# Turning 32x32 blocks into whole transposes: a round trip through DRAM against sixteen direct transfers inside SBUF

## The chip, the core and the metric

The kernel runs on one core of one Trainium2 chip. The time is the device time of one execution in microseconds (us), and lower is better. The core has TensorE (PE) for matrix products, with its own row for weight loads (PEld), VectorE (DVE), ScalarE (ACT), GpSimd (POOL) and SyncE (SP), which here only issues transfers. PE writes to the accumulation memory PSUM; everything else lies in the on-chip memory SBUF (128 partitions) or in DRAM.

## What is computed

Two layers over x of shape (1, 256, 2048): h = h + Mixer(RMSNorm(h)). Layer A is a gated DeltaNet, layer B a banded softmax attention. Both have 16 heads of 128 features, one wide input projection (8224 and 8192 columns) and an output projection of 2048 x 2048. Cut to its core, the reference is:

```python
def gated_deltanet(h, ...):                       # layer A
    proj = h @ w_in
    qkv = silu(causal_depthwise_conv(proj[..., :6144], conv_w))
    q, k, v = heads of qkv;  q, k = l2_norm(q), l2_norm(k)
    # chunks of 64: decay products, a unit lower triangular solve, a scan over chunks
    o = rms_norm(o, out_norm_w) * silu(z)
    return o @ w_out

def chunk_band_attention(h, ...):                 # layer B
    q, k = rms_norm(heads), rms_norm(heads);  v, z = proj parts
    s = q @ k.T * scale + bias[relative distance]  # own chunk and 8 before it
    o = softmax(s) @ v
    return (o * silu(z)) @ w_out
```

Everything is float32. The kernel splits each weight tile and each activation into a high part (float32r) and the rest, and adds three products.

## The kernel before

**The weight stream.** The list `plan` (L137 to L159) holds all weight tiles, 512 KB each, in order of use; one tile with its matmuls is called a chunk, and `state["use"]` counts them. For each chunk SP loads a tile into `wt` (four buffers, L203), ACT copies its high part to `whi` (L204) and DVE writes the rest to `wlo` (L205); both have three buffers. PE then runs 12 products of width 512 in a "tokens" chunk, whose result has tokens on partitions, or 16 in a "half" chunk (widths 512 and 256), whose result has features on partitions (L253).

**The work between.** All other work is written as generators in two lanes, `bgq` and `bg2`. `tick` and `step` (L225 to L246) advance one of them by one step after a part of each chunk, so their instructions are emitted between the matmuls. `until(n)` holds a generator until chunk n has been reached; such numbers are called distances here. A planner orders the instructions of each engine when the program is built (L1375): it simulates the engines and takes, in the order of emission, what it believes to be ready. On the chip each engine then runs its list strictly in order, and waits at an instruction whose data are not there.

**The turn.** In several places a [tokens, features] array has to become [features, tokens] or the reverse. DVE's transpose turns 32x32 blocks in place of a whole 128x128 transpose, so the blocks lie transposed but on the wrong partitions: block (r, c) still stands at partition group r and has to go to partition group c. Before the change this is done by `trip` (L410), where POOL writes the whole array to a DRAM buffer, and `back` (L417), where SP reads it in four transfers, one for each group of 32 partitions:

```python
nc.gpsimd.dma_start(out=m, in_=u.rearrange("p x c j -> p c (x j)"))            # trip
nc.sync.dma_start(out=dst[32 * c:32 * c + 32].rearrange("i r x j -> i r (x j)"),  # back, c = 0..3
                  in_=m[:, c, :].rearrange("(r i) y -> i r y", r=4))
```

Between the two stands a distance, and another one between `back` and the instruction that reads the result. There are 29 such turns: four in `v_conv` (layer A's values; the turned blocks lie in the tile `raw`, of which there is one, and `v_turn` at L859 reads the result), two in `ha_land` (first layer's output, L1023), four in `zb_small` (layer B's gates; `z`), eight in `qk_norm` (k straight into `kn`; q into a landing tile that ACT scales into `qn`, L1148), eight in `attend` (the softmax weights of two heads at a time; the turned blocks lie in one single buffer, `st["u"]`, which L1193 writes) and three in `out_land` (the last output, L1294). The landing tiles have the tag `cv`, which has two buffers. In `attend` a head goes through the stages scores, weights, turned and fetched_, two chunks apart. POOL also computes the powers that the norms need: `rn` (L1124) in `qk_norm`, `ro` (L907) in `v_gate`.

Of the kernel before, what the change touches and what calls it, by code (L numbers as in the profile page):

```python
# [7 lines left out]
F32 = mybir.dt.float32  # L8
# [6 lines left out]
P = 128  # L15
# [24 lines left out]
def tile_hybrid_trunk(  # L40
# [11 lines left out]
    nc = tc.nc  # L52
# [13 lines left out]
    def wk(tag, bufs=None):  # L66

        return work.tile([P, 4, T], F32, name=tag, tag=tag, bufs=bufs)
# [91 lines left out]
    fetched, splits, state = {}, {}, {"next": 0, "use": 0, "mm": None}  # L160
# [52 lines left out]
    bgq, bg2, now = [], [], []  # L213
# [191 lines left out]
    beta = ht("beta")  # L405
    rows = ctx.enter_context(tc.tile_pool(name="rows", bufs=1, space=bass.MemoryType.DRAM))

    trips = [0]

    def trip(u):  # L410

        trips[0] += 1
        m = rows.tile([P, 4, 32 * u.shape[1]], F32, name="trip%d" % trips[0])
        nc.gpsimd.dma_start(out=m, in_=u.rearrange("p x c j -> p c (x j)"))  # L414
        return m

    def back(dst, m):  # L417

        for c in range(4):
            nc.sync.dma_start(out=dst[32 * c:32 * c + 32].rearrange("i r x j -> i r (x j)"),  # L420
                              in_=m[:, c, :].rearrange("(r i) y -> i r y", r=4))

    def until(use):

        while state["use"] < use:
            yield 0
# [108 lines left out]
    def conv(src, i0):  # L535

        raw = wk("raw", 1)
        scaled(raw, src, scales["x"][1])
        cv = wk("cv")
        yield cv  # L540
        for i in range(4):
            act.activation(out=cv[:, i, :], in_=raw[:, i, :], func=AF.Copy, scale=conv_w(i0 + i, 3))  # L542
            for s in (1, 2, 3):
                dve.scalar_tensor_tensor(out=cv[:, i, s:], in0=raw[:, i, :T - s], scalar=conv_w(i0 + i, 3 - s),  # L544
                                         in1=cv[:, i, s:], op0=ALU.mult, op1=ALU.add)
            yield cv
# [280 lines left out]
    def v_conv(gi, ps):  # L827
        for n, cv in enumerate(conv(ps, 32 + 4 * gi)):
            if n in (2, 4):
                act.activation(out=cv[:, n - 2:n], in_=cv[:, n - 2:n], func=AF.Silu)  # L830
            yield 1
        u = wk("raw", 1).rearrange("p h t -> p (h t)").rearrange("p (c x j) -> p x c j", c=4, j=32)
        for n in (0, 2):
            dve.transpose(out=u[:, 2 * n:2 * n + 4],
                          in_=cv[:, n:n + 2].rearrange("p h (t c i) -> p (h t) c i", t=2, c=4))
            yield 1
        m, end = trip(u), state["use"]
        yield from until(end + 4)
        while vmem["turned"] < gi - 1:
            yield 0  # L840
        land = wk("cv").rearrange("p h t -> p (h t)").rearrange("p (r x j) -> p r x j", r=4, j=32)
        back(land, m)
        vmem[gi] = land
        yield 1

# [169 lines left out]

    def ha_land(ks, u, end):
        yield from until(end)
        m, end = trip(u), state["use"]
        yield from until(end + 4)
        land = wk("cv").rearrange("p h t -> p (h t)").rearrange("p (r x j) -> p r x j", r=4, j=32)  # L1020
        back(land, m)
        yield from until(end + 7)
        h = hmem["h"][:, ks, :].rearrange("p k (t r j) -> p (k t) r j", t=2, r=4)  # L1023
        dve.tensor_tensor(out=h, in0=land.rearrange("p r x j -> p x r j"), in1=h, op=ALU.add)
        yield 1
        yield from ha_split(ks)
# [15 lines left out]
    bmem = {}  # L1042
# [36 lines left out]
    def zb_small(gi, ps, end):  # L1079
        n, u = wk("cv").rearrange("p h t -> p (h t)").rearrange("p (t d) -> p t d", t=2), blocks(8)  # L1080
        for t in range(2):
            act.activation(out=n[:, t, :], in_=ps[:, t, :], func=AF.Silu, scale=scales["h"][0][:, t:t + 1])
        yield 1

        bias, hs = bmem["bias"], slice(4 * gi, 4 * gi + 4)
        dve.tensor_copy(out=bias[0:1, 4 * gi, 0:1], in_=n[0:1, 0, 0:1])
        nc.gpsimd.dma_start(out=bias[:, hs, :], in_=relb[:, hs, :])
        pool.memset(bias[0:64, hs, 192:256], NEG)
        yield 1
        for t in range(2):  # L1090
            turn_tokens(u, t, n[:, t, :])
            yield 1
        m = trip(u)
        yield from until(end + 4)
        back(bmem["z"][:, gi], m)
        yield 1

    while "x" not in hmem:
        step()
# [10 lines left out]
    for j in (2, 3):  # L1110
        bgq.append(zb_small(j, block("tokens", xb, 2), state["use"]))

    def qk_norm(ps, scale, dst, end):

        ssn = tiny.tile([P, 2, 4], F32, name="ssn", tag="so")
        rn = tiny.tile([P, 2, 4], F32, name="rn", tag="ro")
        sq = wk("cv").rearrange("p h t -> p (h t)")
        act.activation(out=sq, in_=ps.rearrange("p t d -> p (t d)"), func=AF.Square)
        yield from until(end + 1)
        dve.reduce_sum(out=ssn, in_=sq.rearrange("p (t h d) -> p t h d", t=2, d=P), axis=AX.X)  # L1120
        for t in range(2):
            pool.tensor_scalar(out=ssn[:, t, :], in0=ssn[:, t, :], scalar1=1.0 / P, scalar2=bmem["uh"][:, t:t + 1],
                               op0=ALU.mult, op1=ALU.add)
        pool.tensor_tensor(out=rn, in0=ssn, in1=nhalf[:, :8].rearrange("p (t h) -> p t h", t=2), op=ALU.pow)  # L1124
        yield from until(end + 3)
        n = wk("cv").rearrange("p h t -> p (h t)").rearrange("p (t d) -> p t d", t=2)
        for t in range(2):
            dve.tensor_tensor(out=n[:, t, :].rearrange("p (h d) -> p h d", d=P),
                              in0=ps[:, t, :].rearrange("p (h d) -> p h d", d=P),
                              in1=rn[:, t, :].unsqueeze(2).broadcast_to([P, 4, P]), op=ALU.mult)  # L1130
        yield 1
        u = wk("cv").rearrange("p h t -> p (h t)").rearrange("p (c x j) -> p x c j", c=4, j=32)
        for t in range(2):
            dve.transpose(out=u[:, 4 * t:4 * t + 4], in_=n[:, t, :].rearrange("p (x c i) -> p x c i", c=4, i=32))
            yield 1
        m = trip(u)
        yield from until(end + 6)
        if scale is None:
            back(dst, m)
            yield 1  # L1140
            return
        g = wk("cv").rearrange("p h t -> p (h t)").rearrange("p (r x j) -> p r x j", r=4, j=32)
        back(g, m)
        yield from until(end + 10)
        while bmem["scored"] < bmem["turned"]:
            yield 0
        bmem["turned"] += 1
        act.activation(out=dst.rearrange("p x (r j) -> p r x j", r=4), in_=g, func=AF.Copy, scale=scale)  # L1148
        yield 1

    def attend(gi, qn, kn, end):
# [5 lines left out]
        st = {}  # L1157
# [31 lines left out]
        def turned(i):  # L1189
            if i % 2 == 0:  # L1190
                st["u"] = hmem["m"][:, 11264:12032].rearrange("p (c x j) -> p x c j", c=4, j=32)
            x = 3 * (i % 2)
            dve.transpose(out=st["u"][:, x:x + 3], in_=st[i][0].rearrange("p (x c i) -> p x c i", c=4, i=32))  # L1193
            if i % 2:
                st["m", i] = trip(st["u"])

        def fetched_(i):
            if i % 2:
                back(weights_of((4 * gi + i) // 2), st["m", i])

        stages = (scores, weights, turned, None, None, fetched_)
        while bmem["turned"] <= gi:
            yield 0
        for n in range(4 + len(stages) - 1):
# [8 lines left out]
    def weights_of(pr):  # L1213

        w = bmem["w"][:, 768 * pr:768 * pr + 768] if pr < 5 else hmem["m"][:, 2 * D + 768 * (pr - 5):2 * D + 768 * (pr - 4)]
        return w.rearrange("p (r x j) -> p r x j", r=4, j=32)
# [31 lines left out]
    for gi in range(4):  # L1248
        c = 1024 * (gi % 2)
# [30 lines left out]
    def out_turn(j, ps, end):  # L1280
        u = blocks(8)
        for t in range(2):
            turn_tokens(u, t, ps[:, t, :])
        yield 1
        bg2.append(out_land(j, trip(u), end))

    def out_land(j, m, end):
        yield from until(end + 3)
        land = wk("cv").rearrange("p h t -> p (h t)").rearrange("p (r x j) -> p r x j", r=4, j=32)
        back(land, m)  # L1290
        yield from until(end + 6)
        ks = slice(4 * j, 4 * j + 4)
        h = h_r[:, ks, :].rearrange("p k (t r j) -> p (k t) r j", t=2, r=4)
        dve.tensor_tensor(out=h, in0=land.rearrange("p r x j -> p x r j"), in1=h, op=ALU.add)  # L1294
        nc.sync.dma_start(out=ov[:, ks], in_=h_r[:, ks, :])
        yield 1
# [82 lines left out]
```

## Time and profile before

| | us |
|---|---|
| median of 3 runs (lowest to highest) | 976.91 (975.65 to 978.31) |
| the profiled execution | 974.92 |
| its span in the profile | 973.2 |
| busy: PE, DVE, ACT, POOL | 967.4, 702.3, 519.7, 91.4 |
| granted TensorE clock in the profiled execution | 1.00 |

The span is what the profile's rows are counted in; 1.7 us of the profiled execution lie outside it. In the rows, "L253" is a line of the kernel, "x24" a count, and "a<-b" says that a is written from b. A wait "X <- Y" is idle time of X that ended when Y was done. "SPq" rows are the transfer commands on SP's list, and their duration is the time that a command takes to issue, not the transfer; the time from issue to landing has its own column.

### The profile page before, as it was taken

The page shows a single profiled execution, that of the slowest core. Times are in us where ns is not written, and L with a number is a line of the kernel's source. Part 1 is how long each engine was busy: PE and PEld are TensorE (multiplying, and loading weights), DVE is VectorE, ACT ScalarE, POOL GpSimd, SP SyncE. Part 2 cuts the span into 40 slices and gives each one's busy share as a digit, 9 for nine tenths or more (in the row PEclk, how much of TensorE's full clock was granted, in tenths as well). Part 3 has the DMA queues.
Part 4 walks back from the last instruction along what each step waited for, and adds up shares of the span by engine and source line. Part 5 has one row for each costly group of instructions (what it writes and reads, how often), then busy time and mean ns, then how long its engine had stood idle before and what let it go on. Part 6 is the DMA issues. An engine that isn't in the chain of part 4 may idle for free.

```text
span 973.2 us, 14443 instructions
## 1 busy us (share of the span) xinstructions
PE 967.4 (99%) x5355; PEld 825.4 (85%) x5355; DVE 702.3 (72%) x1147; ACT 519.7 (53%) x731; POOL 91.4 (9%) x126
## 2 busy tenths in 40 slices
PE   9999999999999999999999999999999999999998
PEld 7988888888888889888888888888888888888887
DVE  7789787998899877866686555566767676655464
ACT  8465887655546556544564444445454545444332
POOL 1002100122000000101001000111212120000000
PEclk9999999999999999999999999999999999999999
DMA  9667765645675665566966798788898987665694
GB/s 297 195 168 230 231 197 164 179 128 177 175 195 150 179 204 165 170 192 193 301 201 199 225 286 291 212 250 259 234 288 246 275 249 208 203 191 173 204 308 151
DMA packets 144934, 207.93 MB, mean 214 GB/s; under 512 B 10320, under 2 KB 87008, under 8 KB 144864
## 3 DMA queue, kind: packets, MB, share of 16 engines
q1 hardware_dynamic: 139152, 186.28, 64.9%
q0 software_dynamic: 5424, 20.47, 6.0%
q8 instruction: 42, 0.69, 0.3%
q10 hardware_dynamic: 288, 0.26, 0.1%
q14 instruction: 28, 0.23, 0.1%
HBM read 190.71 MB, written 16.27 MB: 213 GB/s over the span
## 4 chain that ended last, share of the span: by engine, by line
PE 94%; DVE 2%; ACT 1%; DMA 1%; issue 1%; SPq 0%; DVEq 0%; ACTq 0%
PE psp L253 85%; PE pss L627 2%; PE pss L253 1%; PE pss L872 1%; PE pss L1166 1%; PE pss L1235 1%; DMA trip<-raw 1%; DVE wlo L205 1%; DVE cv L544 1%; DMA g<-in_xT_dram 1%; PE pss L893 0%; PE pss L894 0%; PE pss L895 0%; PE pss L879 0%; PE pss L1237 0%
## 5 line engine op out<-in xcount | busy, mean ns | idle before, releaser
L205 DVE TENSOR_TENSOR wlo<-wt,whi 128x1024 fp32r<-128x1024 f32 (+2 forms) x324 | 390.0, 1207 | 206.7 <-ACT whi L204 201.8
L204 ACT CAST whi<-wt 128x1024 fp32r<-128x1024 f32 (+2 forms) x324 | 336.6, 1040 | 366.6 <-PE psp L253 301.8
L253 PE MATMUL psp<-whi,xb 128*128 128x512 f32 x1280 | 402.2, 392 | 0.0
L253 PEld LDWEIGHTS psp<-whi,xb 128*128 128x128 f32 x1280 | 240.0, 188 | 49.2
L253 PE MATMUL psp<-wlo,xb 128*128 128x512 f32 x640 | 249.8, 390 | 0.0
L253 PE MATMUL psp<-xb,whi 128*128 128x512 f32 (+1 forms) x832 | 196.2, 376 | 0.5 <-ACT whi L204 0.5
L253 PEld LDWEIGHTS psp<-xb,whi 128*128 128x128 f32 x832 | 148.2, 189 | 25.2 <-ACT whi L204 0.7
L253 PEld LDWEIGHTS psp<-wlo,xb 128*128 128x128 f32 x640 | 120.2, 188 | 24.6
L253 PE MATMUL psp<-xb,wlo 128*128 128x256 f32 x768 | 113.4, 285 | 0.5 <-DVE wlo L205 0.4
L253 PEld LDWEIGHTS psp<-xb,wlo 128*128 128x128 f32 x768 | 103.3, 191 | 5.0 <-DVE wlo L205 1.1
L253 PE MATMUL psp<-whi,g 128*128 128x512 f32 x320 | 99.5, 390 | 0.0
L253 PEld LDWEIGHTS psp<-whi,g 128*128 128x128 f32 x320 | 60.1, 188 | 12.3
L544 DVE SCALAR_TENSOR_TENSOR cv<-raw,sm,cv 128x255 f32<-128x255 f32 (+2 forms) x144 | 64.3, 480 | 2.4 <-ACT cv L542 2.0
L253 PE MATMUL psp<-wlo,g 128*128 128x512 f32 x160 | 62.7, 392 | 0.0
L253 PE MATMUL psp<-g,whi 128*128 128x512 f32 x160 | 38.5, 391 | 0.0
L253 PEld LDWEIGHTS psp<-wlo,g 128*128 128x128 f32 x160 | 30.0, 188 | 6.2 <-DVE wlo L205 0.3
L253 PEld LDWEIGHTS psp<-g,whi 128*128 128x128 f32 x160 | 29.4, 188 | 5.7
L542 ACT ACTIVATE cv<-raw,sm 128x256 f32<-128x256 f32 x48 | 22.2, 501 | 18.7 <-DVE raw L339 18.7
L414 POOL DMA_DIRECT2D trip<-cv x17 | 9.8, 576 | 147.5 <-DVE cv L434 117.4
L1179 ACT ACTIVATE raw<-raw,mx 128x128 f32<-128x128 f32 (+1 forms) x32 | 14.4, 449 | 16.7 <-DVE mx L1177 16.7
L253 PEld LDWEIGHTS psp<-g,wlo 128*128 128x128 f32 x160 | 20.5, 191 | 0.8
L253 PE MATMUL psp<-g,wlo 128*128 128x256 f32 x160 | 20.8, 283 | 0.0
(251 smaller groups left out, 788.4 us busy)
## 6 DMA issues: line engine op xcount, KB each, us to landing
wt<-in_b_w_in_dram SPq DMA_DIRECT2D x128, 512.0 KB, 4.5
wt<-in_a_w_in_dram SPq DMA_DIRECT2D x125, 512.0 KB, 4.1
wt<-in_a_w_out_dram SPq DMA_DIRECT2D x32, 512.0 KB, 4.9
wt<-in_b_w_out_dram SPq DMA_DIRECT2D x32, 512.0 KB, 4.5
trip<-cv POOLq DMA_DIRECT2D x17, 512.0 KB, 4.5
cv<-trip SPq DMA_DIRECT2D x52, 128.0 KB, 5.0
trip<-dl POOLq DMA_DIRECT2D x8, 384.0 KB, 4.4
tt<-line POOLq DMA_DIRECT2D x4, 512.0 KB, 8.5
```

Of the source, the lines that this page charges most:

```text
L204: cast = act.copy(out=hi[:, js, cs], in_=wt[:, js, cs])
L205: rest = dve.tensor_tensor(out=lo[:, js, cs], in0=wt[:, js, cs], in1=hi[:, js, cs].bitcast(F32), op=ALU.subtract)
L253: state["mm"] = pe.matmul(*args, **kw).ins
L414: nc.gpsimd.dma_start(out=m, in_=u.rearrange("p x c j -> p c (x j)"))
L542: act.activation(out=cv[:, i, :], in_=raw[:, i, :], func=AF.Copy, scale=conv_w(i0 + i, 3))
L544: dve.scalar_tensor_tensor(out=cv[:, i, s:], in0=raw[:, i, :T - s], scalar=conv_w(i0 + i, 3 - s), in1=cv[:, i, s:], op0=ALU.mult, op1=ALU.add)
L627: pe.matmul(dst, lhsT=kq[:, a, i, c:c + P], rhs=rhs, start=(n == 0), stop=(n == 2))
L872: pe.matmul(ps[:, i * P:(i + 1) * P], lhsT=tt[:, 2 * (h0 + i) + t, :], rhs=vb[:, i, t, :], start=True, stop=True)
L1166: pe.matmul(ps[:, 128:384].rearrange("p (t r j) -> p t r j", t=2, j=32), lhsT=q1, rhs=kb, start=True, stop=True)
L1179: act.activation(out=s[:, a:b], in_=s[:, a:b], func=AF.Exp, bias=mx[:, t:t + 1], accum_out=sums[:, t:t + 1])
L1235: pe.matmul(ps[:, 0:256].rearrange("p (x r j) -> p x r j", x=2, j=32), lhsT=v[:, 0, vs], rhs=pT0, start=True, stop=False)
```

## The change

`trip`, `back` and the 29 DRAM buffers go. `regroup` takes their place: for each pair (r, c) one transfer moves the block straight from partition group r of the turned array to partition group c of the destination, 32 partitions with one contiguous run each (1 KB, or 768 B in `attend`). The 16 transfers go in turn to SP and to POOL, eight each. `regroup` is itself a generator: it emits four transfers, then gives the turn back, four times; only `attend` emits all 16 at once. The distances between trip and back fall away, and those before the consumer become shorter where there are any (q: `end + 8` for `end + 10`; output: `end + 5` for `end + 6`; first layer's output: three chunks after the transfers were emitted). In `attend` the stage `fetched_` is gone, and the transfers are issued in the stage `turned`, three stages earlier.

```diff
--- before.py
+++ after.py
@@ -405,20 +405,12 @@
     beta = ht("beta")
     rows = ctx.enter_context(tc.tile_pool(name="rows", bufs=1, space=bass.MemoryType.DRAM))
 
-    trips = [0]
-
-    def trip(u):
-
-        trips[0] += 1
-        m = rows.tile([P, 4, 32 * u.shape[1]], F32, name="trip%d" % trips[0])
-        nc.gpsimd.dma_start(out=m, in_=u.rearrange("p x c j -> p c (x j)"))
-        return m
-
-    def back(dst, m):
-
-        for c in range(4):
-            nc.sync.dma_start(out=dst[32 * c:32 * c + 32].rearrange("i r x j -> i r (x j)"),
-                              in_=m[:, c, :].rearrange("(r i) y -> i r y", r=4))
+    def regroup(dst, u):
+
+        for r in range(4):
+            for c in range(4):
+                (nc.sync, nc.gpsimd)[(r + c) % 2].dma_start(out=dst[32 * c:32 * c + 32, r], in_=u[32 * r:32 * r + 32, :, c])
+            yield 1
 
     def until(use):
 
@@ -834,12 +826,10 @@
             dve.transpose(out=u[:, 2 * n:2 * n + 4],
                           in_=cv[:, n:n + 2].rearrange("p h (t c i) -> p (h t) c i", t=2, c=4))
             yield 1
-        m, end = trip(u), state["use"]
-        yield from until(end + 4)
         while vmem["turned"] < gi - 1:
             yield 0
         land = wk("cv").rearrange("p h t -> p (h t)").rearrange("p (r x j) -> p r x j", r=4, j=32)
-        back(land, m)
+        yield from regroup(land, u)
         vmem[gi] = land
         yield 1
 
@@ -1015,11 +1005,9 @@
 
     def ha_land(ks, u, end):
         yield from until(end)
-        m, end = trip(u), state["use"]
-        yield from until(end + 4)
         land = wk("cv").rearrange("p h t -> p (h t)").rearrange("p (r x j) -> p r x j", r=4, j=32)
-        back(land, m)
-        yield from until(end + 7)
+        yield from regroup(land, u)
+        yield from until(state["use"] + 3)
         h = hmem["h"][:, ks, :].rearrange("p k (t r j) -> p (k t) r j", t=2, r=4)
         dve.tensor_tensor(out=h, in0=land.rearrange("p r x j -> p x r j"), in1=h, op=ALU.add)
         yield 1
@@ -1090,10 +1078,7 @@
         for t in range(2):
             turn_tokens(u, t, n[:, t, :])
             yield 1
-        m = trip(u)
-        yield from until(end + 4)
-        back(bmem["z"][:, gi], m)
-        yield 1
+        yield from regroup(bmem["z"][:, gi], u)
 
     while "x" not in hmem:
         step()
@@ -1133,15 +1118,12 @@
         for t in range(2):
             dve.transpose(out=u[:, 4 * t:4 * t + 4], in_=n[:, t, :].rearrange("p (x c i) -> p x c i", c=4, i=32))
             yield 1
-        m = trip(u)
-        yield from until(end + 6)
         if scale is None:
-            back(dst, m)
-            yield 1
+            yield from regroup(dst, u)
             return
         g = wk("cv").rearrange("p h t -> p (h t)").rearrange("p (r x j) -> p r x j", r=4, j=32)
-        back(g, m)
-        yield from until(end + 10)
+        yield from regroup(g, u)
+        yield from until(end + 8)
         while bmem["scored"] < bmem["turned"]:
             yield 0
         bmem["turned"] += 1
@@ -1192,13 +1174,10 @@
             x = 3 * (i % 2)
             dve.transpose(out=st["u"][:, x:x + 3], in_=st[i][0].rearrange("p (x c i) -> p x c i", c=4, i=32))
             if i % 2:
-                st["m", i] = trip(st["u"])
-
-        def fetched_(i):
-            if i % 2:
-                back(weights_of((4 * gi + i) // 2), st["m", i])
-
-        stages = (scores, weights, turned, None, None, fetched_)
+                for _ in regroup(weights_of((4 * gi + i) // 2), st["u"]):
+                    pass
+
+        stages = (scores, weights, turned, None, None, None)
         while bmem["turned"] <= gi:
             yield 0
         for n in range(4 + len(stages) - 1):
@@ -1282,13 +1261,12 @@
         for t in range(2):
             turn_tokens(u, t, ps[:, t, :])
         yield 1
-        bg2.append(out_land(j, trip(u), end))
-
-    def out_land(j, m, end):
-        yield from until(end + 3)
+        bg2.append(out_land(j, u, end))
+
+    def out_land(j, u, end):
         land = wk("cv").rearrange("p h t -> p (h t)").rearrange("p (r x j) -> p r x j", r=4, j=32)
-        back(land, m)
-        yield from until(end + 6)
+        yield from regroup(land, u)
+        yield from until(end + 5)
         ks = slice(4 * j, 4 * j + 4)
         h = h_r[:, ks, :].rearrange("p k (t r j) -> p (k t) r j", t=2, r=4)
         dve.tensor_tensor(out=h, in0=land.rearrange("p r x j -> p x r j"), in1=h, op=ALU.add)
```

## The prediction

> **What bounds the kernel now.** I read the busy table first, then the table by stretches, to see whether the full PE hides gaps.
>
> ```profile
> span 973.2 us, 14443 instructions
> PE 967.4 (99%) x5355; PEld 825.4 (85%) x5355; DVE 702.3 (72%) x1147; ACT 519.7 (53%) x731; POOL 91.4 (9%) x126
> ```
>
> ```profile
> 300.00:320.00 20.00, 20.00 (x218) 17.44 (x218) 19.52 (x29) 13.84 (x18) 2.75 (x3) 1.00 0.52 139
> 320.00:340.00 20.00, 19.89 (x360) 16.91 (x359) 16.43 (x28) 10.30 (x18) 0.00 (x0) 1.00 0.60 182
> 340.00:460.00 120.00, 120.00 (x724) 104.73 (x723) 87.74 (x141) 65.10 (x91) 10.07 (x9) 1.00 0.60 182
> 560.00:580.00 20.00, 20.00 (x90) 16.57 (x89) 10.07 (x10) 7.89 (x9) 0.84 (x2) 1.00 0.95 293
> 700.00:720.00 20.00, 20.00 (x90) 16.57 (x89) 13.34 (x16) 9.70 (x10) 4.22 (x5) 1.00 1.01 299
> 960.00:973.00 13.00, 9.79 (x62) 8.69 (x61) 6.14 (x9) 1.62 (x3) 0.00 (x0) 1.00 0.24 82
> ```
>
> The columns are stretch, length, then busy time and count of PE, PEld, DVE, ACT and POOL, the granted clock, the transfer engines' share and GB/s. PE works through every stage in which a turn happens: 0.11 us idle between 300 and 460 us, none at 560 or at 700. Of the 5.8 us that PE is idle in all (973.2 - 967.4), 3.2 lie in the last stretch, at the kernel's end. So whatever becomes earlier can give back almost nothing; the question is which delay reaches PE.
>
> Where would it? In the chain of waits one turn lies on the path:
>
> ```profile
> 318.05 6.10 DMA trip<-raw
> 324.24 0.70 DVE raw L339
> ...
> 337.29 4.91 PE psp L253 x25
> ```
>
> Start, duration, work. Between 300 and 320 us DVE is 19.52 of 20 busy, because the triangular solve's end, the values' convolution and the weight split meet there. DVE stands at L339 until the single tile `raw` has been read out to DRAM, and from there the path runs through DVE's list back to PE's stream at 337.29. The other stages have a reserve, read from DVE's and ACT's lists in order of time:
>
> ```profile
> 690.88 0.57 DVE L1193 STREAM_TRANSPOSE dl<-raw 128x384 f32<-128x384 f32 x1
> 696.12 1.29 DVE L1128 TENSOR_TENSOR cv<-psp,rn 128x512 f32<-128x512 f32 x2 [1.16 <-POOL rn L1124]
> 698.46 0.57 DVE L1193 STREAM_TRANSPOSE dl<-raw 128x384 f32<-128x384 f32 x1
> 700.20 1.19 DVE L205 TENSOR_TENSOR wlo<-wt,whi 128x1024 fp32r<-128x1024 f32 x1
> 709.22 1.22 DVE L205 TENSOR_TENSOR wlo<-wt,whi 128x1024 fp32r<-128x1024 f32 x1 [1.49 <-ACT whi L204]
> ```
> ```profile
> 697.29 1.06 ACT L204 CAST whi<-wt 128x1024 fp32r<-128x1024 f32 x1 [0.79 <-ACT raw L1179]
> 705.41 1.05 ACT L204 CAST whi<-wt 128x1024 fp32r<-128x1024 f32 x1 [1.66 <-PE psp L253]
> 708.13 1.05 ACT L204 CAST whi<-wt 128x1024 fp32r<-128x1024 f32 x1 [1.67 <-PE psp L253]
> 571.64 2.16 ACT L204 CAST whi<-wt 128x1024 fp32r<-128x1024 f32 x2 [3.94 <-DMA wt<-in_b_w_in_dram]
> ```
>
> A chunk takes 2.72 us (705.41 to 708.13). A cast begins when PE frees one of three buffers, so its tile is needed two chunks later: 708.13 + 5.44 = 713.57. DVE's part of it is done at 710.44, which is 3.1 us early. A weight that came 3.94 us late (571.64) cost PE nothing: the stretch 560 to 580 shows 20.00. So delays of up to about 3 us on DVE, and of 4 us on a load, are covered.
>
> **The change, part by part.** The prices:
>
> ```profile
> L414 POOL DMA_DIRECT2D trip<-cv x17: 533/559/617, 462.9 to 949.1; - x17
> L414 POOL DMA_DIRECT2D trip<-dl x8: 542/544/550, 691.8 to 847.3; - x8
> L414 POOL DMA_DIRECT2D trip<-raw x4: 531/566/682, 318.1 to 408.3; - x4
> L420 SPq DMA_DIRECT2D cv<-trip x52: 303/430/1442, 324.2 to 954.5; - x52
> L859 DVEq EVENT_SEMAPHORE  x8: 21/36/50, 329.8 to 417.6; - x8
> ```
> ```profile
> trip<-cv POOLq DMA_DIRECT2D x17, 512.0 KB, 4.5
> kT<-trip SPq DMA_DIRECT2D x20, 96.0 KB, 3.3
> line<-kT POOLq DMA_DIRECT2D x1, 16.0 KB, 2.8
> ```
> ```profile
> SPq L420 <- DMA trip<-cv: 36.5, 17, 4.6
> SPq L420 <- DMA trip<-dl: 11.7, 8, 2.0
> SPq L420 <- DMA trip<-raw: 9.0, 4, 4.6
> ```
>
> The first fence has minimum, median and maximum in ns of an issue; the second KB each and the median us from issue to landing; the third SP's waits in all, their number, the longest.
>
> *Removed:* 29 POOL issues and 116 SP issues, SP's 57.2 us of standing (36.5 + 11.7 + 9.0) with weight loads queued behind it, and half the bytes: 21 x 512 KB + 8 x 384 KB out and the same back become one move. *Worth:* nothing. SP's longest stand, 4.6 us, is inside the reserve of a load, and PE shows no gap there.
>
> *Added on SP:* 232 issues for 116, that is 8 x 0.43 = 3.4 us a turn instead of 1.7. A load behind them is at most 3.4 us later, less than the covered 3.94. They wait for DVE's transposes instead of a landing. Price 0, covered by four weight buffers; without that cover 3.4 us a turn.
>
> *Added on POOL:* 232 issues for 29. A turn takes POOL 8 x 0.56 = 4.5 us instead of 0.56, in all 203 x 0.56 = 114 us on an engine with 91.4 busy. That matters where the last piece's landing is waited for, or where POOL owes DVE something. No row shows a 32 KB piece's landing; the bounds are 2.8 us (16 KB from POOL) and 4.5 us (512 KB from POOL). I take 3.3, the 96 KB row, which is the nearest one out of this pattern.
>
> *First values turn (318 us, on the path).* Last piece starts 7 x 0.566 = 4.0 us after the first and lands 3.3 later: 7.3 us instead of 6.10, so +1.2 (bounds 4.0 + 2.8 - 6.1 = +0.7 and 4.0 + 4.5 - 6.1 = +2.4). The consumer now collects 16 completions instead of one; at 36 ns per collecting instruction 15 more are 0.5 us on DVE. Together **+1.7**, bounds 0 (the planner puts other DVE work first, and the wait has no one behind it) and +2.9. The later three values turns land earlier than before (no DRAM hop), so these waits shrink:
>
> ```profile
> DVE dl L859 <- DMA cv<-trip: 8.0, 3, 4.2
> DVE raw L339 <- DMA trip<-raw: 3.2, 1, 3.2
> ```
>
> At PE's 120.00 of 120 the 8.0 us are worth nothing.
>
> The Trainium skill ("DMA: Bandwidth & Descriptors", Rules for kernel authors) speaks against the change: it says to coalesce small transfers, because under 64 KB one pays mostly overhead, and the same page (Anatomy of one DMA, SWDGE path) puts about 2.0 us of fixed cost on each transfer. As an estimate from that page a 32 KB piece lands in 2.1 us; since pieces overlap, this term would be 4.0 + 2.1 - 6.1 + 0.5 = +0.5 and the sum, by the profiled execution's time, 974.9 + 0.5 = 975.4. Were the 2 us paid one after another, a turn's eight pieces would hold POOL's queue for 17 us; the 16 KB row's 2.8 us is of the first kind, and no run here shows pieces in a row.
>
> *Attention turns (eight, `attend`).* All 16 pieces are emitted at once, and the single buffer `st["u"]` is written again two chunks later. I price this at 0 in the forecast, because the planner draws DVE's list anew and may put the rewrite behind weight splits; the upper bound is the first rival.
>
> *Gates, q and k, outputs.* In the gates POOL's pieces stand behind a memset that waits for a bias load, and the next gate's transposes reuse the buffer two chunks later:
>
> ```profile
> 558.84 0.31 POOL L1088 MEMSET dl<- 64x256 f32 x1 [4.08 <-DMA dl<-in_relb_dram]
> 560.18 0.71 DVE L434 STREAM_TRANSPOSE cv<-cv 128x512 f32<-128x512 f32 x1 [2.05 <-DMA trip<-cv]
> ```
>
> The transposes already stand 2.05 us here; with eight pieces behind 558.84 the last lands 0.3 + 4.0 + 3.3 us on, at 566.4. That would be 6 us more if the next gate came as early as now, but it is emitted only after the four steps of `regroup`, some two chunks later, so I count no loss (bound +2.5). Elsewhere the pieces go out two per step and engine, and readers come two chunks (5.4 us) or more behind the last piece, against 3.3 to 4.5 of landing. Shorter distances put them at the edge, so waits of 1 to 2 us may appear on DVE or ACT; the 3.1 us cover them. Price 0; without cover 15 such turns would cost up to 2 us each.
>
> **Sum:** 974.92 (the profiled execution: span 973.2 and 1.7 around it) + 1.7 = 976.6. The median of the runs is 976.91, 2.0 above that execution, so the forecast is 976.91 + 1.7 = **978.6**.
>
> **Rivals.** *First, slower: POOL's queue in the attention stage.* The rows that collide:
>
> ```profile
> 691.75 0.55 POOL L414 DMA_DIRECT2D trip<-dl  x1 [16.11 <-DVE sums L1185]
> 692.73 1.61 POOL L1122 TENSOR_SCALAR ssn<-ssn,uh 128x4 f32<-128x4 f32 x2 [0.42 <-DVE ssn L1120]
> 694.42 1.66 POOL L1124 TENSOR_TENSOR rn<-ssn,nhalf 128x8 f32<-128x8 f32 x1
> ```
>
> One issue stands right before the power `rn`, for which DVE already waits 1.16 us at 696.12. If all eight go first, the last starts at 691.75 + 7 x 0.544 = 695.6 and `rn` is 3.8 us late: DVE stands 5.0. If the power goes between them, the last piece starts 3.3 us later, at 698.9, and lands by 701.7 to 703.4, while DVE reaches its rewrite at 698.46: it stands 3.2 to 4.9. The reserve there is smaller than 3.1, since the split at 700.20 ends at 701.39 for a tile whose cast began at 697.29 and which is needed at 702.73: 1.3 us. PE loses 1.9 to 3.6 us (3.2 - 1.3 to 4.9 - 1.3; the first order's 3.8 - 1.3 lies between) for each of the three head groups that have a next q, 5.7 to 10.8 in all. With the first turn's 1.7 that is +7.4 to +12.5; I take the lower third, +9: **986**. It decides once DVE stands there longer than 1.3 us more than before. For it speaks that the planner judged landings too early before (three waits at L859, 29 of SP at L420); against it, that a list drawn with 16 pieces in it moves the rewrite back.
>
> *Second: nothing reaches PE.* The planner fills DVE at 318 us with weight splits, the pieces land as the 16 KB row does, and the time stays at **976.9**. For it: PE lost only 0.11 us although DVE stood 3.2 us at L339. Lower it can hardly go.
>
> *Third: loads held by the pieces.* A load has been seen to wait for a landing of an earlier transfer of SP's list:
>
> ```profile
> SPq L178 <- DMA cv<-trip: 0.6, 3, 0.3
> ```
>
> If such waits grow with 16 pieces so that a load in each of the eight attention turns comes 3.4 + 1.1 = 4.5 us late, that is 0.6 over the covered 3.94; 8 x 0.6 + 1.7 gives +6.5: **983.4**. Against it: half the bytes leave the transfer engines, which are full there now (1.01).
>
> **How the numbers follow.** Chances: forecast 0.44, POOL's queue 0.30, nothing 0.18, held loads 0.08. A change under 0.3% (2.9 us here) can't be told from none. The forecast's own range is 976.3 to 979.8; most of it counts as same, a tenth lies beyond. Same: 0.9 x 0.44 + 0.85 x 0.18 + 0.03 from small versions of the others, about 0.57; slower: 0.38; faster: 0.05, for a median that falls low by itself, as PE has no more than 0.11 us to give between 300 and 460. The range runs from 975.0 (the runs' own lowest is 975.65) to 988.0, which takes in most of the first rival.
>
> **What would show it.** Right: PE's busy time within 2 us of 967.4, DVE's wait at L339 near 320 us 4 to 5 us instead of 3.2, SP's 57 us at the round trip gone, POOL's row near 205 us. Wrong: a stretch between 660 and 800 us where PE is under 20.00 with DVE's L1193 or L1128 before it (first rival), or ACT's casts waiting over 4 us for loads with PE idle (third). A time below 974 would mean that PE's own pace depends on the transfers, which nothing here shows.

## The result, and the profile after

The changed kernel takes **983.25 us** (median of 6 runs) against 977.03 for the kernel before in the same session: a ratio of **1.0065**, 95% interval 1.0043 to 1.0086. It is slower by about 6 us. The forecast was 978.6, a change too small to measure; the measured time is 4.65 us above it, slower as forecast, and inside the range of 975.0 to 988.0. The delay came from elsewhere than the forecast had it.

The changed kernel's first profile is of a disturbed execution (5551.82 us), so all rows "after" are of a repeat of the same kernel: 983.69 us, ratio 1.0069 (1.0050 to 1.0087), span 982.2. First its busy table:

```profile
span 982.2 us, 15076 instructions
PE 971.0 (99%) x5355; PEld 827.4 (84%) x5355; DVE 701.3 (71%) x1147; ACT 520.0 (53%) x731; POOL 189.8 (19%) x329
```

PE is still at 99%, which hides the loss, as it hid the gaps before. The table by stretches shows the place (columns as in the prediction). Before:

```profile
300.00:460.00 160.00, 159.89 (x1298) 139.08 (x1298) 123.70 (x196) 89.24 (x126) 12.83 (x12) 1.00 0.59 177
660.00:800.00 140.00, 140.00 (x630) 116.31 (x630) 100.98 (x187) 70.97 (x107) 25.98 (x30) 1.00 0.86 256
```

After:

```profile
300.00:460.00 160.00, 160.00 (x1305) 139.97 (x1304) 124.22 (x197) 89.74 (x127) 27.12 (x40) 1.00 0.56 165
...
660.00:800.00 140.00, 134.54 (x588) 110.38 (x587) 91.70 (x174) 66.38 (x99) 54.39 (x94) 0.98 0.66 203
```

Count the matmuls. Between 660 and 800 us PE finishes 588 instead of 630. At 140 / 630 = 0.222 us each, the missing 42 are 9.3 us, and the spans differ by 982.2 - 973.2 = 9.0. So all that the two profiles differ by was lost in the attention stage. Of the 9.3 us, 140.00 - 134.54 = 5.5 are idle. The other 3.9 are, for the most part, matmuls that ran at a lower clock (0.98 on average; the last section has the places). The medians differ by less than the profiles, 6.2 us, since the profiled execution of the kernel before (974.92 us) is 2 us faster than its median.

What was PE waiting for? The waits in all (total, times, longest), then PE's and ACT's lists in order of time:

```profile
PE psp L253 <- ACT whi L204: 4.0, 2, 2.2
PE psp L253 <- DVE wlo L205: 2.6, 5, 0.8
ACT whi L204 <- DMA wt<-in_b_w_in_dram: 33.3, 13, 8.0
```
```profile
719.81 1.04 ACT L204 CAST whi<-wt 128x1024 fp32r<-128x1024 f32 x1 [7.98 <-DMA wt<-in_b_w_in_dram]
720.90 0.50 PE L253 MATMUL psp<-whi,xb 128*128 128x512 f32 x1 [2.24 <-ACT whi L204]
722.16 0.80 PE L253 MATMUL psp<-wlo,xb 128*128 128x512 f32 x1 [0.76 <-DVE wlo L205]
...
774.44 0.50 PE L253 MATMUL psp<-whi,xb 128*128 128x512 f32 x1 [1.71 <-ACT whi L204]
775.70 0.50 PE L253 MATMUL psp<-wlo,xb 128*128 128x512 f32 x1 [0.76 <-DVE wlo L205]
```

A weight tile comes late, its cast waits 7.98 us, and PE stands until the high part, and again until the rest, is there: 2.24 + 0.76 + 1.71 + 0.76 = 5.47 us, the whole idle time of the stretch. Why was the tile late? SP's list around the first place, after:

```profile
696.22 6.20 SPq L178 DMA_DIRECT2D wt<-in_b_w_in_dram  x4
704.19 2.41 SPq L412 DMA_DIRECT2D kT<-dl  x4
706.97 5.66 SPq L412 DMA_DIRECT2D cv<-cv  x8
712.67 2.50 SPq L412 DMA_DIRECT2D kT<-dl  x4
715.27 2.13 SPq L178 DMA_DIRECT2D wt<-in_b_w_in_dram  x4
```

Before:

```profile
704.64 2.22 SPq L420 DMA_DIRECT2D cv<-trip  x4
706.96 1.18 SPq L178 DMA_DIRECT2D wt<-in_b_w_in_dram  x2
709.21 1.75 SPq L420 DMA_DIRECT2D kT<-trip  x4
```

Two turns meet here: the second turn of an attention group (`kT<-dl`) and the turn of the next group's q (`cv<-cv`). Their pieces on SP form **one row of 16**, from 704.19 to 715.17, without a single weight load. Before, loads stood between the two turns. Behind the row SP issues four loads in 2.13 us without a wait, so their buffers had come free while the row ran: it was the row that held them. In the chain of waits the row is seen piece by piece, and it ends in the load that PE needed:

```profile
714.57 0.60 SPq L412
715.27 4.43 DMA wt<-in_b_w_in_dram
719.81 1.05 ACT whi L204
```

### The profile page after: what moved, and what is told of

Same layout as the page of the kernel before. It is cut to its first block, busy times and chain, and to the rows that moved or that the text cites. A ratio compares the mean times of both kernels' runs of the same rounds, so it can differ in the third digit from the quotient of the medians.

```text
span 5550.1 us, 15076 instructions
## 1 busy us (share of the span) xinstructions
PE 5545.7 (100%) x5355; PEld 4128.0 (74%) x5355; DVE 714.1 (13%) x1147; ACT 524.3 (9%) x731; POOL 178.4 (3%) x329
## 3 DMA queue, kind: packets, MB, share of 16 engines
HBM read 176.56 MB, written 2.11 MB: 32 GB/s over the span
## 4 chain that ended last, share of the span: by engine, by line
PE 100%; DVE 0%; issue 0%
PE psp L253 90%; PE pss L619 2%; PE pss L253 1%; PE pss L862 1%; PE pss L1214 1%; PE pss L1148 1%; PE pss L885 0%; PE pss L1216 0%; PE pss L869 0%; PE pss L883 0%; PE pss L934 0%; PE pss L884 0%; PE pss L1147 0%; PE pss L755 0%; PE pss L90 0%; PE pss L759 0%
## 5 line engine op out<-in xcount | busy, mean ns | idle before, releaser
L253 PE MATMUL psp<-whi,xb 128*128 128x512 f32 x1280 | 1947.8, 1703 | 0.0
L253 PEld LDWEIGHTS psp<-whi,xb 128*128 128x128 f32 x1280 | 1168.4, 914 | 511.3 <-issue 511.3
L253 PE MATMUL psp<-wlo,xb 128*128 128x512 f32 x640 | 1092.3, 1707 | 0.0
L253 PE MATMUL psp<-xb,whi 128*128 128x512 f32 (+1 forms) x832 | 1063.0, 1593 | 0.0
L253 PEld LDWEIGHTS psp<-xb,whi 128*128 128x128 f32 x832 | 731.1, 920 | 242.5 <-issue 241.1
L253 PEld LDWEIGHTS psp<-wlo,xb 128*128 128x128 f32 x640 | 584.3, 913 | 254.2 <-issue 254.2
L253 PEld LDWEIGHTS psp<-xb,wlo 128*128 128x128 f32 x768 | 549.8, 929 | 37.7 <-issue 37.7
L253 PE MATMUL psp<-xb,wlo 128*128 128x256 f32 x768 | 556.2, 1036 | 0.0
L253 PE MATMUL psp<-whi,g 128*128 128x512 f32 x320 | 485.8, 1699 | 0.0
L253 PEld LDWEIGHTS psp<-whi,g 128*128 128x128 f32 x320 | 292.5, 915 | 127.5 <-issue 127.5
L412 POOL DMA_DIRECT2D cv<-cv x72 | 35.4, 500 | 732.8 <-DVE cv L426 557.4
```

Source lines behind the costliest of these rows:

```text
L253: state["mm"] = pe.matmul(*args, **kw).ins
L412: (nc.sync, nc.gpsimd)[(r + c) % 2].dma_start(out=dst[32 * c:32 * c + 32, r], in_=u[32 * r:32 * r + 32, :, c])
```

## The experiments

Runs 1 to 4 were set up with three theories: *POOL's queue* (the prediction's first rival; eight pieces stand ahead of the power `rn`), *values* (the stage at 318 us) and *clock* (a lower clock in all stages). *SP's row* (16 pieces in a row hold a weight load; the "SP theory" of the expectations below) came out of the profile of run 1, which is the one shown above. That profile speaks against two of them: between 300 and 460 us PE did more matmuls than before, not fewer, at a clock of 1.00. This left SP's row against POOL's queue. The order of instructions that POOL's queue needs is really there, POOL's list first, then DVE's:

```profile
691.43 3.91 POOL L412 DMA_DIRECT2D kT<-dl  x8 [12.50 <-DVE sums L1167]
...
697.03 1.66 POOL L1109 TENSOR_TENSOR rn<-ssn,nhalf 128x8 f32<-128x8 f32 x1
```
```profile
701.93 1.28 DVE L1113 TENSOR_TENSOR cv<-psp,rn 128x512 f32<-128x512 f32 x2
703.13 1.03 DVE L1175 STREAM_TRANSPOSE dl<-raw 128x384 f32<-128x384 f32 x2
```

But the planner put DVE's reader of `rn` (L1113) and the rewrite of `st["u"]` (L1175) behind weight splits, and neither waits. Lines after the change are 10 to 18 lower (L859 is now L849, L1128 is L1113, L1193 is L1175); the pieces are L412, and L427 in kernels that keep `trip`.

**1. The changed kernel once more,** with no edit.

> The changed kernel once more, unaltered, for a profile of an undisturbed execution. All theories: 982 to 985 us against 976 to 978 for the kernel before. Queue theory (POOL's eight issues stand in front of the power rn and of DVE's rewrite of the attention buffer): PE idles or stretches mainly between 660 and 800 us, DVE's wait for rn is 4 us or more in three places. Values theory (the stage at 318 us, where DVE is full): most of the 6 us lie between 305 and 345 us. Clock theory (TensorE's granted clock is lower with this kernel): the clock column shows about 0.996 to 0.998 and 2 to 4 us of the 6 are spread over all stages in proportion to the clock.

983.69 us (983.06 to 986.89), ratio 1.0069. The loss is repeatable.

**2. The attention's eight turns back through DRAM,** the other 21 direct:

```diff
-                for _ in regroup(weights_of((4 * gi + i) // 2), st["u"]):
-                    pass
+                st["m", i] = trip(st["u"])       # and back() in the stage fetched_
```

> The changed kernel with its eight attention turns put back to the round trip through DRAM (one POOL write, four SP reads three stages later); the other 21 turns stay direct. Queue theory: the loss is gone, 976 to 979 us. Values theory: it stays at 982 to 984 us. Clock theory: it stays near 982 with the clock under 1.

977.1 us, ratio 0.9996 (0.9984 to 1.0008). The other 21 turns, with 168 pieces on each of the two engines, cost nothing that the medians show; the loss needs the attention's pieces. (The profiled execution, 977.63 us, does show a little: between 660 and 800 us PE stands 1.7 us for late weight parts.) The values and clock theories had 982 to 984 us here.

**3. The kernel before, with only the attention's turns direct:**

```diff
-                st["m", i] = trip(st["u"])       # back() in fetched_
+                for _ in regroup(weights_of((4 * gi + i) // 2), st["u"]):
+                    pass
```

> The kernel before with only its eight attention turns made direct (16 pieces each, issued in the stage turned). Queue theory: the loss is here, 981 to 985 us. Values theory: 976 to 978 us.

978.13 us, ratio 1.0013 (1.0000 to 1.0026). So the attention's pieces do not cost the 6 us by themselves either, as POOL's queue had it (981 to 985). Taken with run 2, two harmless halves make a harmful whole: something must come from their meeting.

**4. All 16 pieces of every turn on SP:**

```diff
-                (nc.sync, nc.gpsimd)[(r + c) % 2].dma_start(...)
+                nc.sync.dma_start(...)
```

> The changed kernel with all 16 pieces of every turn on SP's list, none on POOL's. A turn then takes SP 16 x 0.43 = 6.9 us. Queue theory: rn comes in time again, so 2 to 6 us of the loss go, unless loads held on SP for 6.9 us (over the 3.9 us that were covered) put 3 us per turn in their place, which would show as ACT waiting for wt and a time of 985 us or more. Values theory: about the same 983 us, as the last piece is issued 6.5 us behind the first instead of 4.

1083.53 us, ratio 1.1078 (1.1054 to 1.1103). Its waits:

```profile
ACT whi L204 <- DMA wt<-in_b_w_in_dram: 125.6, 26, 18.2
PE psp L253 <- ACT whi L204: 57.5, 18, 12.2
```

Late loads grow with the rows on SP, as SP's row says.

**5. The attention's pieces all on POOL,** the others split as in the changed kernel, and **6. all pieces on POOL:**

```diff
-    def regroup(dst, u):
+    def regroup(dst, u, qs=(nc.sync, nc.gpsimd)):     # run 6: nc.gpsimd for all
-                (nc.sync, nc.gpsimd)[(r + c) % 2].dma_start(...)
+                qs[(r + c) % 2].dma_start(...)
-                for _ in regroup(weights_of((4 * gi + i) // 2), st["u"]):
+                for _ in regroup(weights_of((4 * gi + i) // 2), st["u"], (nc.gpsimd, nc.gpsimd)):
```

> The changed kernel with the 16 pieces of each attention turn all on POOL's list; the other turns stay split between SP and POOL. SP theory (16 pieces that stand in one row on SP's list, issued at 0.62 us each, hold the weight loads for 11 us, twice between 700 and 780 us; PE idles and its granted clock drops behind the gap): no more than eight pieces stand in a row on SP, so the loss goes, 976 to 978.5 us, the ACT waits for loads stay under 4 us. Queue theory (POOL's pieces in front of rn and of the rewrite): POOL now has 8 us of pieces in front, so 984 to 992 us.

> The changed kernel with all 16 pieces of every turn on POOL's list, none on SP's. SP theory: loads are never held by pieces, so ACT waits for loads no more than in the kernel before; what remains is POOL's own delay of the powers and of the landings (8 us a turn instead of 4), for which I expect 977 to 982 us. Queue theory: 990 us or more, PE idle behind rn. All on SP took 1083.5 us.

1005.17 us, ratio 1.0285 (1.0265 to 1.0305), and 1030.34, ratio 1.0546 (1.0528 to 1.0565). Here the numbers of SP's row fell (976 to 978.5 and 977 to 982 us): with SP relieved the time got worse, not better. POOL's queue had 984 to 992 and at least 990. In run 5, POOL's and DVE's lists and PE's waits:

```profile
691.46 5.39 POOL L412 DMA_DIRECT2D kT<-dl  x11 [12.69 <-DVE sums L1167]
...
703.43 1.67 POOL L1109 TENSOR_TENSOR rn<-ssn,nhalf 128x8 f32<-128x8 f32 x1
```
```profile
710.08 1.03 DVE L1175 STREAM_TRANSPOSE dl<-raw 128x384 f32<-128x384 f32 x2
711.03 1.25 DVE L1113 TENSOR_TENSOR cv<-psp,rn 128x512 f32<-128x512 f32 x2
```
```profile
PE psp L253 <- DVE cv L1113: 13.6, 4, 4.1
...
ACT whi L204 <- DMA wt<-in_b_w_in_dram: 9.8, 4, 3.2
```

`rn` starts 6.4 us later than in the changed kernel (703.43 for 697.03), DVE reads `psp` 9.1 us later (711.03 for 701.93), and PE waits for that accumulator; the lines left out between the two of POOL's list hold the other five pieces, so all 16 stand ahead of `rn`. ACT's longest wait for these loads is 3.2 us, less than a load's cover, so it is a third path, which begins like POOL's queue and ends elsewhere: **POOL late, so `rn` late, so an accumulator in PSUM is freed late.** These waits are 13.6 us of a loss of some 29; the rest was not followed up, nor was run 6. Run 5 says nothing against SP's row in the changed kernel; it shows that POOL has no room for twice the pieces. Whether eight on POOL already cost something needed another run (9).

**7. The kernel before, plus one row of 16 extra pieces on SP** in each of the four attention groups (32 partitions x 128 B, from `st["u"]` to an unused buffer, in one unbroken row), and **8. the same pieces without the order,** so that the planner may put loads between them:

```diff
+            if i == 3:
+                for r in range(4):
+                    for c in range(4):
+                        queued(spare[32 * c:32 * c + 32, r], st["u"][32 * r:32 * r + 32, 0, c])
+                        # run 8: nc.sync.dma_start(...) in place of queued(...)
```

> The kernel before, with its round trips, and once per head group 16 more small transfers on SP's list (32 partitions x 128 B inside SBUF, into a tile that nobody reads), chained so that they stand in one row between two weight loads. They are extra work and change nothing else. SP theory: four rows of 16 x 0.62 = 9.9 us; each keeps a load 4 to 6 us beyond the covered 4, so PE idles 1 to 3 us and loses as much again by the clock: 982 to 992 us. Queue theory: POOL's list and DVE's waits are as before, so 976 to 978 us.

> The same 4 x 16 extra transfers on SP's list, not chained, so that the planner puts them two to four at a time between the weight loads. SP theory: the number of issues is the same, but no load is held more than 2.5 us, so 976 to 978.5 us. If the number of transfers on SP or their traffic costs PE, as much as with the row of 16.

In one row: 980.58 us, ratio 1.0037 (1.0024 to 1.0049), less than the theory had given it. Spread: 978.66, ratio 1.0019 (1.0006 to 1.0033). In run 7 the row and PE's gap behind it are:

```profile
713.11 1.46 SPq L178 DMA_DIRECT2D wt<-in_b_w_in_dram  x2
715.56 12.39 SPq L178 DMA_DIRECT2D spare<-dl  x16
```
```profile
733.59 0.50 PE L253 MATMUL psp<-whi,xb 128*128 128x512 f32 x1 [1.36 <-ACT whi L204]
734.85 0.50 PE L253 MATMUL psp<-wlo,xb 128*128 128x512 f32 x1 [0.76 <-DVE wlo L205]
```

A row on SP, with nothing else changed, makes the same kind of gap. It is smaller (2.12 us, then 2.09). A likely reason is that two loads were issued right before the row, while in the changed kernel nothing but the row was issued from 702.42 on; no run tests it. The spread pieces cost about half by the medians (0.0019 x 976.3 = 1.9 us), so the number of pieces may have a small price of its own. But the intervals of the two runs overlap a little, and the profiled execution of run 8, its fastest (975.80 us), shows no idle PE between 660 and 800 us, so where the 1.9 us go is open.

A row of 16 does not always cost. The changed kernel has a third one, from 813.34 to 823.55 us; there the longest wait of a cast for its load is 3.12 us, and PE is busy throughout (16.00 of 16 us from 812 to 828). In run 7, too, only the first two of its four rows leave a gap; behind the third (813.59 to 825.54) and the fourth PE is busy 100.00 of 100 us, from 800 to 900. What the later places have in reserve was not looked into.

**9. The changed kernel with the next q's four turns back through DRAM,** and **10. with only the second attention turn of each group (four of 29) back through DRAM.** Each takes away one half of the row:

```diff
+        m = trip(u)                              # run 9, in qk_norm, q only
+        yield from until(end + 6)
         g = wk("cv")...
-        yield from regroup(g, u)
-        yield from until(end + 8)
+        back(g, m)
+        yield from until(end + 10)
```
```diff
-            if i % 2:                            # run 10, in attend
+            if i == 1:
                 for _ in regroup(weights_of((4 * gi + i) // 2), st["u"]):
                     pass
+            if i == 3:
+                st["m"] = trip(st["u"])          # and back() in the stage fetched_
```

> The changed kernel with the next q's four turns back through DRAM; the attention's eight turns, k, gates, values and outputs stay direct. Theory (SP's row: the second attention turn and the next q's turn stand in one row of 16 pieces, which holds the next weight load by some 10 us): with the q's 8 pieces gone the longest row on SP is 8, or 5 us, and the load is at most 1 to 2 us late, which ACT's casts cover: 976.5 to 978.5 us, PE at 139 or more of 140 between 660 and 800. Rival (POOL's queue: pieces ahead of the power rn): the attention's 8 pieces on POOL still stand ahead of rn, so the loss stays, 981 to 985 us.

> The changed kernel with only the second attention turn of each head group (four of 29 turns) back through DRAM; the first stays direct, the q's turns too. Theory (SP's row of 16): the row is cut from its other side, so most of the loss goes: 976.5 to 979 us, with PE at 139 or more of 140 between 660 and 800. Rival (the direct attention turns cost each by itself, whatever stands beside them): half of them are left, so half of the loss is: 979.5 to 981 us.

Run 9: 975.13 us, ratio 0.9982 (0.9973 to 0.9991). Run 10: **974.47 us, ratio 0.9974 (0.9964 to 0.9984)**. With either half taken away, the whole loss is gone. Run 10's SP list and its stretch:

```profile
706.96 4.95 SPq L427 DMA_DIRECT2D cv<-cv  x8
712.01 2.28 SPq L178 DMA_DIRECT2D wt<-in_b_w_in_dram  x3
714.38 2.23 SPq L420 DMA_DIRECT2D kT<-trip  x4
```
```profile
660.00:800.00 140.00, 140.00 (x631) 116.37 (x630) 99.98 (x187) 70.63 (x107) 53.57 (x86) 1.00 0.75 230
```

Three loads stand between the two turns again. And run 9 rules out the pieces ahead of `rn` as the cause, since POOL issues them there as in the changed kernel:

```profile
691.72 3.91 POOL L427 DMA_DIRECT2D kT<-dl  x8 [12.70 <-DVE sums L1184]
...
697.39 1.66 POOL L1124 TENSOR_TENSOR rn<-ssn,nhalf 128x8 f32<-128x8 f32 x1
```

Runs 9 and 10 also take half of the same two turns' pieces off POOL's list. That it is SP's half that counts is seen in the changed kernel's trace, where PE and the casts wait for loads, which SP issues, and in run 7, where POOL's list is as before.

Both kernels came out below what the theory had given them (976.5 at the least), and below the kernel before. The profile shows only 0.3 us of that (spans 972.9 and 973.2). The rest lies in the runs: those of run 10 reach from 973.99 to 975.83, those of the kernel before from 975.40 to 980.25. What makes its longer runs long was not profiled and stays open.

**11. The attention's pieces handed out over four steps** in place of all 16 at once:

```diff
-                for _ in regroup(weights_of((4 * gi + i) // 2), st["u"]):
-                    pass
+                bg2.insert(0, regroup(weights_of((4 * gi + i) // 2), st["u"]))
```

> The changed kernel with the attention's pieces handed out over four steps of the background list, as the other turns are, instead of all 16 at once. Theory (SP's row of 16): weight loads get between the pieces, the longest row falls to 8 or less and the loss shrinks: 976.5 to 980 us. It can be worse if the pieces, being later, hold the rewrite of the single buffer u (DVE's transposes wait for them): then 983 to 990 us, with DVE's wait at the transposes of the attention's weights. Rival (the number of pieces alone, not their order, costs the time): no change, 982 to 986 us.

983.32 us, ratio 1.0071 (1.0053 to 1.0088): no gain, where the theory's number was 976.5 to 980. SP's list says why:

```profile
703.91 2.41 SPq L412 DMA_DIRECT2D kT<-dl  x4
706.68 6.09 SPq L412 DMA_DIRECT2D cv<-cv  x8
712.82 2.50 SPq L412 DMA_DIRECT2D kT<-dl  x4
```

The edit changed the order in which the pieces are emitted, but the planner set them into the same row. So the run did not test what it was made for; it shows that the same row costs the same time.

## What of the prediction held, and which step failed

The direction and the range came out, and the mechanism did not. That the time lies inside the range is luck: its upper end was set for the first rival, which did not decide.

*"Added on SP ... 8 x 0.43 = 3.4 us a turn ... Price 0."* **This step failed,** in two ways. The issue times, minimum/median/maximum in ns, after:

```profile
L412 SPq DMA_DIRECT2D kT<-dl x40: 507/588/1674, 691.2 to 802.4; - x40
L412 POOL DMA_DIRECT2D kT<-dl x40: 496/496/587, 691.4 to 801.4; - x40
```

A piece takes SP 0.59 us, not 0.43, which was read from the reads out of DRAM; eight take 4.95 us. Larger was the second error: I priced each turn alone, with the cover of 3.94 us for each, and did not ask which turns stand next to each other on SP. Two of them made 715.17 - 704.19 = 11.0 us without a load, three times the 3.4. The cover was real (rows of eight cost nothing in runs 9 and 10); it was used twice in one place. The 3.94 us themselves are only the longest wait of a cast that had been seen to cost nothing: in run 9 a row of eight took 7.66 us (from 737.86) without any idle PE between 660 and 800 us.

*Third rival, loads held by the pieces, chance 0.08, price 983.4.* This is the mechanism that decided, and its sign in the trace came as written (casts that wait over 4 us for loads, with PE idle). Its price was near the measured time by accident: 8 x 0.6 + 1.7 was worked out, with 1.1 us in the 4.5 for which no row is given, while the profile shows two places with 5.5 us of idle PE and 3.9 of slower work behind them, and 0.3 gained elsewhere. Its chance was far too low, because I tied it to waits for landings and not to the issue time itself. The point against it, half the bytes, was true (writes to DRAM fell from 16.27 to 2.11 MB) and no help: the tile was late in being issued, not in landing. It took 4.43 us to land, as others do.

*First values turn, +1.7.* Did not come. DVE's wait at L339 is gone: in the new list it comes at 330.83 us instead of 324.24, and neither it nor the reader of the landing (L849) waits:

```profile
329.62 1.29 DVE L849 TENSOR_TENSOR dl<-cv,rk 128x512 f32<-128x512 f32 x2
330.83 1.29 DVE L339 TENSOR_TENSOR raw<-ev,rB 128x512 f32<-128x512 f32 x2
```

PE did 1305 matmuls between 300 and 460 us instead of 1298. This is the second rival ("nothing reaches PE"), right for this stage; run 2 at 0.9996 shows it, by the median, for all 21 turns outside the attention.

*Attention turns priced at 0 because the planner redraws DVE's list.* Right for DVE, as L1113 and L1175 above show; the price lay on SP. The first rival (chance 0.30) saw the right stage and the right order on POOL, but wrong consequences: with eight pieces no one waits. With 16 (run 5) it becomes real, by way of the accumulator instead of the buffer.

*POOL's row near 205 us:* 189.8, since a piece takes 0.50 us instead of 0.56. *SP's standing at the round trip:* gone, as foreseen; no run prices it alone, but run 2, where most of it is gone, is no faster than the kernel before. *PE within 2 us of 967.4:* 971.0, so this sign speaks against the forecast, as it should.

The Trainium skill ("DMA: Bandwidth & Descriptors", Issuing engines are not separate DMA queues) says that starting transfers on several engines saves only the sequencer's time for issuing them, which it calls usually small beside the transfer. One piece agrees: it takes SP 0.59 us, against 3.2 us (median) from issue to landing. A row does not: 16 pieces held SP for 11.0 us. And who issues counts here: 983.7 us (split), 1083.5 (SP alone), 1030.3 (POOL alone).

## What to carry to other kernels

When one long transfer is replaced by many short ones, price the rows in which they will stand on the issuing queue, all users of that queue taken together, against the time for which the queue's next important transfer can wait; a price for each group alone is not enough. The mix of run 10 has the lowest median here (974.47 us, 0.9974 of before; the profiles differ by only 0.3 us): direct transfers everywhere, except where two turns fall into the same gap between loads. And a row on another engine is no free place: POOL had room for eight pieces ahead of its small power instruction, not for 16.

## What the runs showed of the hardware

**A short PE gap can cost more than its length.** The granted clock (after the counts of the five engines) behind the first and second gap of the changed kernel:

```profile
720.00:724.00 4.00, 2.34 (x5) 1.69 (x6) 2.84 (x3) 2.95 (x3) 0.00 (x0) 0.73 0.83 287
724.00:728.00 4.00, 4.00 (x16) 3.25 (x15) 1.34 (x2) 1.59 (x2) 0.00 (x0) 0.85 0.93 334
728.00:732.00 4.00, 4.00 (x19) 3.30 (x19) 3.07 (x3) 2.50 (x4) 1.21 (x2) 1.00 0.53 160
...
776.00:780.00 4.00, 4.00 (x12) 3.10 (x11) 2.21 (x2) 1.05 (x1) 0.00 (x0) 0.57 0.90 273
```

Behind the smaller gap of run 7, and behind the second gap of run 11:

```profile
736.00:740.00 4.00, 4.00 (x20) 3.30 (x19) 3.05 (x10) 1.48 (x2) 0.00 (x0) 1.00 1.04 380
776.00:780.00 4.00, 4.00 (x18) 3.31 (x19) 2.59 (x3) 2.40 (x3) 0.00 (x0) 1.00 0.90 278
```

After gaps of 2.24 + 0.76 and 1.71 + 0.76 us the clock fell, and 16 and 12 matmuls fit into 4 us instead of 18 to 20; after 1.36 + 0.76 us it stayed at 1.00. The length alone does not decide: after 1.75 + 0.76 us in run 11, at the same place and a little longer than the gap of 1.71 + 0.76, it stayed at 1.00 too. What decides was not shown. Behind the first gap the clock was back at 1.00 by 728 to 732. The three stretches below 1.00 come to 4 x (0.27 + 0.15 + 0.43) = 3.4 us, most of the 3.9 beside the 5.5 of standing. The Trainium skill ("TensorE: Matmul & The Clock Gate", What's actually happening) has the clock halved after one idle window of about 3.4 us and full again after about as long of work, with a window that runs freely. The return agrees; the length does not, since none of these gaps reaches 3.4 us.

**The price of an issue depends on the form of the transfer.** On SP a piece inside SBUF (24 or 32 KB) took 0.59 us where a read of 128 KB out of DRAM took 0.43; on POOL 0.50 where a write of 512 KB to DRAM took 0.56. A small transfer is not cheaper to issue because it is small: a weight load of 512 KB took SP 0.37.
